# Some loads and stores of the decoder step moved from SyncE's DMA queue to GpSimd's, two blocks not fetched twice, gate weights split later

## The chip, the cores and the metric

The kernel runs on one core of a Trainium2 chip. The metric is the device time of one execution in microseconds, the median of several runs.

## What is computed

One inference step of a two-layer decoder with 2048 prompt positions and 32 sample positions (8 sequences of 4), model width 1024. Layer 0 is gated linear attention, layer 1 a sliding-window attention over one shared K/V. Cut to what matters:

```python
u = rmsnorm(h, norm_g)                       # layer 0
q, k, v, gate, g_low = split(u @ a_w_in)     # widths 512, 512, 2048, 2048, 16
log_a = log_sigmoid(g_low @ a_w_gate2 + a_b_gate) / 16
o, state = gla_recurrence(q, k, v, log_a)    # 4 heads, chunks of 64
h = h + (rmsnorm(o) * silu(gate)) @ a_w_out  # 2048 -> 1024
k, v = shared_kv(h)                          # 4 KV heads of 64
q, gate = split(rmsnorm(h, b_norm) @ b_w_in) # layer 1, 32 heads of 64
o = banded_attention(q, k, v, window=128, sinks)
y = h + (o * silu(gate)) @ b_w_out           # 2048 -> 1024
```

The same is done for the sample positions (`ys`), and the recurrent states and K/V caches are further outputs.

## The kernel before

Values are carried as pairs of 16-bit numbers (a high and a low half), so a product takes three matmul passes, and every weight is loaded raw in 32 bits, split by ScalarE (high half) and VectorE (low half) at L197 and L198, and then multiplied. Transposed operands are made by transposing DMAs, all of them on SyncE's queue.

The stages, in order of time. (1) **The start**, 0 to about 60 us: the first 512 positions of `x_prompt` are loaded (`u_steps`, L382) and normed in four chunks of 128 (`norm_T`: a square sum on ScalarE and VectorE, the reciprocal root on GpSimd as `rs_m`, `rs_r` at L186 and L187, the scaled halves into `ogT`, two transposes `uT<-ogT` at L322), the first head's weights are loaded and split (`Unit.convert`, L223), and the low-rank gate's weights `wg` are split by GpSimd (`split_wg`). (2) **Layer 0**, to about 1150 us, with 36 weights of layer 1 prepared on the side (`pre<-pst` stores on GpSimd's queue). (3) **The form stage**, about 1150 to 1410 us: `a_out` makes layer 0's output projection for 16 chunks of 128 positions. Each chunk fetches four transposed blocks (`sg<-ogd` or `v<-ogd`, L1059, the two names in turn), multiplies, adds the residual on VectorE (L1066, one half of the columns at a time, with `X` loaded at L1064), stores `hd` (L1067) and norms the chunk. Beside it `form_steps` prepares layer 1's output weights: the output projection of layer 1 takes chunks in pairs by a scheme of seven products in place of eight, for which seven combinations of four weight blocks are formed. For each of 8 steps `m` it loads four blocks of 256 KB of `b_w_out` (L857; two `wraw`, one `qT`, one `kT`, these two with one buffer each), subtracts four times on GpSimd (L864), splits seven times on ScalarE and VectorE, and stores seven results in `wfd` from GpSimd's queue (L878). (4) **Layer 1**, to about 2500 us: four groups of 16 blocks, TensorE's order written out by hand in `ORDER`. (5) **The tail**, from about 2500 us: the first products of the pairs, the sample's output (`s_out`, `b_finish_s`, L1664 to L1670), and pairs 0 to 7. A pair needs four blocks (`load`, `fetch`, transposes `<-oge` at L1569), sums of them on VectorE (`sums`: `whole` L1583, L1595, L1600, L1601, L1609), seven products of 24 matmuls, and for each of four results an `hd` load (L1625), two adds (L1626, L1618) and a store of `y` (L1627).

What sets the order: the Tile scheduler orders each engine's instructions, each engine and each DMA queue then works in that order, so an instruction that waits holds all behind it on its queue. `behind(..., 200)` lowers the priority of a list of steps; `later` is a DMA that keeps its place in the program. `trickle` and `summing` hand out single steps of the first pair's loads, weight fetches and sums between the last blocks of layer 1, and `run(trickle + summing)` does what is left of them. `wform_big` (L1533) fetches a formed weight into a `uT` buffer (four quarters of 512 KB), `wform` (L1538) into `W` buffers. Product n=6 of a pair uses weight 6, which `wform_big` fetches into the buffer `t_` that holds four blocks (0 to 3) fetched earlier for the first products.

Of the kernel before, what the change touches and what calls it, by code (L numbers as in the profile page):

```python
# [19 lines left out]
P = 128  # L20
# [54 lines left out]
def _body(tc, nc, cp, sb, ps, dr, i, o):  # L75
# [88 lines left out]
    def run(steps):  # L164
        for f in steps:
            f()
# [23 lines left out]
    def split(dst, src, sc=None, eng=dve):  # L190
# [5 lines left out]
        else:  # L196
            act(hi, src, AF.Copy, scale=sc)  # L197
            dve.scalar_tensor_tensor(lo, src, sc, hi, ALU.mult, ALU.subtract)  # L198

    class Unit:  # L200


# [9 lines left out]
        def convert(self, half, dst):  # L212

            ncol, gs = self.ncol, self.gs
            nk = 512 // ncol
            raw = T("wraw", [P, 512], F32, 3)
            for n, (off, w, src) in enumerate(self.parts):
                if self.groups:
                    g, z = self.groups, len(self.parts)
                    to = raw.rearrange("p (g z d) -> p z g d", z=z, g=g)[:, n]  # L220
                    nc.sync.dma_start(to, src[half * P : (half + 1) * P].rearrange("p (g d) -> p g d", g=g))
                    continue
                nc.sync.dma_start(  # L223
                    raw.rearrange("p (k c) -> p k c", c=ncol)[:, :, off : off + w],
                    src[half * nk * P : (half + 1) * nk * P].rearrange("(k p) c -> p k c", p=P),
                )
            if gs is None:
                split((dst(0), dst(1)), raw, SW)
                return
            for n in range(nk):  # L230
                d = slice(n * ncol, (n + 1) * ncol)
                k = self.kts[half * nk + n]
                split((dst(0)[:, d], dst(1)[:, d]), raw[:, d], gs[:, k : k + 1])
# [92 lines left out]


    wg_raw = T("E", [P, KT, RANK], F32, 2)
    nc.scalar.dma_start(wg_raw, i["a_w_in"][0, :, 5120:5136].rearrange("(k p) c -> p k c", p=P))
    wg = T("ogTs", [P, KT, 6 * RANK], F16, 1)  # L330
    w2 = T("w2", [6 * RANK, 512], F16, 1)
    gl = T("gl", [6 * RANK, NBL, 512], F16, 1)
# [516 lines left out]
    def form_steps(m):  # L849

        b, f = {}, {}

        def load():
            for n, (r, z) in enumerate(((0, 0), (0, 1), (1, 0), (1, 1))):
                t = T(("wraw", "wraw", "qT", "kT")[n], [P, 512], F32, 3 if n < 2 else 1)
                k = UP[m] + 2 * r
                nc.sync.dma_start(t, i["b_w_out"][0][k * P : (k + 1) * P, z * 512 : z * 512 + 512])  # L857
                b[r, z] = t
            f[0], f[3], f[5] = b[0, 0], b[1, 0], b[1, 1]

        def put(n):
            def sub(x, y):
                t = T("sth", [P, 512], F32, 2)
                pool.tensor_tensor(t, x, y, ALU.subtract)  # L864
                f[n] = t

            if n == 2:
                sub(b[0, 1], b[0, 0])
            elif n == 1:
                sub(b[1, 1], f[2])  # L870
            elif n == 4:
                sub(b[1, 1], b[0, 1])
            elif n == 6:
                sub(b[1, 0], f[1])
            t = T(tags[0], [P, 2, 512], F16, 2)
            tags.append(tags.pop(0))
            split((t[:, 0], t[:, 1]), f[n], SWB)
            nc.gpsimd.dma_start(wfd[n][:, m], t)  # L878

        return behind([load] + [lambda n=n: put(n) for n in (0, 2, 1, 3, 6, 5, 4)], 200)  # L880
# [26 lines left out]
    qk_chunk, qk_fin = cur.qk_first()  # L907
    first = u_steps(0)
    qkw = [f for u in hw[0].qk for f in u.steps()]
    run([first[0]] + qkw[:2] + [first[1]] + qkw[2:] + first[2:4])  # L910
    split_wg()
    run(hw[0].v.steps())
    load_w2()
# [640 lines left out]
    class Pair:  # L1554
# [66 lines left out]
        def y(self, c, half, pp, t):  # L1621

            cs = slice(half * 512, half * 512 + 512)
            hr = T("E", [P, 512], F32, 2)
            nc.sync.dma_start(hr, hd[c][:, cs])  # L1625
            dve.tensor_tensor(hr, hr, t, ALU.add)  # L1626
            nc.sync.dma_start(o["y"][0, c * P : (c + 1) * P, cs], self.add("st", pp, hr))  # L1627

        def steps(self, n):
            tag, w = PRODS[n]  # L1630
# [33 lines left out]
    def b_finish_s(half, pt):  # L1664
        cs = slice(half * 512, half * 512 + 512)
        hr = T("E", [SMP, 512], F32, 2)
        nc.sync.dma_start(hr, hsd[:, cs])
        y = T("st", [SMP, 512], F32, 2)
        dve.tensor_tensor(y, pt, hr, ALU.add)
        nc.sync.dma_start(o["ys"].flatten_outer_dims()[:, cs], y)  # L1670

    blks = []
    parts = {}
# [12 lines left out]
    for t in range(-3, NKV * NCH):  # L1686
        fill = []
        n = t + 3
# [34 lines left out]
        if n == TOT - 11:  # L1723
            t_ = T("uT", [P, 8, 8, P], F16, 4)
            for x in range(4):
                pr = pairs[x // 2]
                pr.l[x % 2] = [t_[:, 2 * x], t_[:, 2 * x + 1]]
                pr.fetch(x % 2, pr.l[x % 2])
        if n in (TOT - 7, TOT - 3):
            run(quarters(wform_big, {TOT - 7: 0, TOT - 3: 2}[n]))  # L1730
        if n == TOT - 14:
            run(quarters(wform, 3))
        if n == TOT - 1:
            trickle += [lambda x=x: pairs[0].load(x) for x in (3, 2, 0, 1)] + quarters(wform_big, 1)
            summing += pairs[0].sums()
        if n == TOT:
            trickle += quarters(wform, 4) + quarters(wform, 5)
        if n == TOT + 1:
            trickle += quarters(wform_big, 6)
        if boundary:  # L1740
            boundary.pop(0)()
    for n, (od, ca) in enumerate((("cks", "cache_swa_k"), ("cvs", "cache_swa_v"))):
# [3 lines left out]
    for n, od in enumerate(("cks", "cvs")):  # L1746
        for b in range(NS):
            nc.sync.dma_start(o[od][b, WIN - TS :], kvS[b * TS : (b + 1) * TS, n])
    run(trickle + summing)
    for p_ in range(NCH // 2):  # L1750
        more = []
        if p_ + 1 < NCH // 2:
# [91 lines left out]
```

## Time and profile before

| | |
|---|---|
| runs of before | 2858.11, 2863.62, 2863.80 us (median 2863.62) |
| profiled execution | 2863.85 us; its span 2862.1 us |
| TensorE busy | 2735.9 us, 96% |
| VectorE, ScalarE, GpSimd busy | 64%, 50%, 37% |
| mean granted TensorE clock | 0.983 of full speed |
| DMA through SyncE's and ScalarE's queues (hardware_dynamic) | 352.75 MB, 54.6% of 16 engines' span |
| DMA through GpSimd's queue (software_dynamic) | 35.66 MB, 3.4% |
| VectorE's last add ends / the span ends | 2858.8 / 2862.1 us |

The span is the time from the first to the last instruction of the profiled execution, 1.75 us shorter than that execution's own time. Share of busy time is an average; what a stage is worth is read from the stretches in which TensorE stands idle.

### The profile page before, as it was taken

Reading aid. Unit: us, or ns where it says so; the run is one execution under the profiler, and the core shown is the slowest. Engines: PE = TensorE matmul, PEld = TensorE weight load, DVE = VectorE, ACT = ScalarE, POOL = GpSimd, SP = SyncE. Lnnn points to the kernel's source line nnn. Section 1 sums busy time; section 2 is a strip of 40 time slices with the busy share of each in tenths; the row PEclk is TensorE's granted clock in tenths of the full one; section 3 lists DMA queues with packets and bytes.
Section 4 is the critical chain, followed back from the end, with each engine's and each line's share of the span. In section 5 each row is a group of like instructions: output and inputs, shape, how many; then the busy total and the mean of one; then the engine's idle time right before and its main releaser. Section 6 shows DMA issues by size and latency. Waiting matters only on the chain.

```text
span 2862.1 us, 51609 instructions
## 1 busy us (share of the span) xinstructions
PE 2735.9 (96%) x19070; PEld 1392.4 (49%) x19070; DVE 1845.7 (64%) x3815; ACT 1440.3 (50%) x3385; POOL 1063.6 (37%) x1471
## 2 busy tenths in 40 slices
PE   6899999999999999999899999999999999988999
PEld 3445444444454444444344555555555555543444
DVE  5767787677768775336413666677777766767653
ACT  6655665466546654333313555566666666641110
POOL 1242233222322321116405676666566556530000
PEclk9899999999999999999999999999999999999999
DMA  8351334124312533799975555866877788798651
GB/s 209 90 124 36 100 101 150 38 82 136 115 38 85 171 84 96 180 240 282 233 193 135 108 130 120 203 117 129 173 116 130 157 155 165 151 236 172 125 112 57
DMA packets 774230, 391.78 MB, mean 137 GB/s; under 512 B 629200, under 2 KB 698776, under 8 KB 773944
## 3 DMA queue, kind: packets, MB, share of 16 engines
q1 hardware_dynamic: 761016, 352.75, 54.6%
q0 software_dynamic: 10880, 35.66, 3.4%
q8 instruction: 149, 2.44, 0.4%
q14 instruction: 105, 0.86, 0.1%
q10 hardware_dynamic: 2080, 0.07, 0.0%
HBM read 138.90 MB, written 107.54 MB: 86 GB/s over the span
## 4 chain that ended last, share of the span: by engine, by line
PE 56%; DVE 12%; DMA 11%; ACT 10%; issue 6%; POOL 4%; SPq 1%; DVEq 0%; ACTq 0%; POOLq 0%
PE pj L101 33%; PE o L101 11%; PE tr L101 8%; PE kv L101 3%; ACT o L1279 2%; DMA pst<-v 2%; DVE v L198 2%; ACT v L197 2%; DMA pre<-pst 1%; PE lev L101 1%; DMA wraw<-in_a_w_in_dram 1%; DVE o L1274 1%; DVE W L198 1%; POOL ogT L195 1%; DVE lev L1274 1%
## 5 line engine op out<-in xcount | busy, mean ns | idle before, releaser
L101 PE MATMUL pj<-W,uT 128*128 128x512 f16 x5088 | 1208.1, 383 | 6.6 <-ACT qT L430 2.9
L101 PEld LDWEIGHTS <-uT 128*128 128x128 f16 x6976 | 654.7, 99 | 714.1 <-issue 40.4
L101 PE MATMUL tr<-W,uT 128*128 128x512 f16 x1536 | 365.8, 379 | 0.0
L186 POOL TENSOR_SCALAR rs_m<-ss 128x1 f32<-128x1 f32 (+3 forms) x190 | 46.1, 243 | 685.7 <-ACT og L611 234.0
L101 PEld LDWEIGHTS <-X 128*128 128x128 f16 x2744 | 185.8, 98 | 149.3 <-issue 14.7
L1279 ACT ACTIVATE o<-o,mx 128x256 f32<-128x256 f32 (+1 forms) x384 | 168.5, 439 | 168.1 <-DVE mx L1274 163.6
L1274 DVE CUSTOM_DVE_ANT_0 o<-o,madd,nsink 128x256 f32<-128x256 f32 (+1 forms) x384 | 184.0, 479 | 48.3 <-PE o L101 44.0
L101 PE MATMUL pj<-uT,W 128*128 128x512 f16 (+1 forms) x912 | 186.0, 354 | 27.0 <-DMA uT<-ogT 24.3
L198 DVE SCALAR_TENSOR_TENSOR v<-o,v 128x512 f16<-128x512 f32 (+1 forms) x192 | 128.8, 671 | 102.0 <-ACT v L197 82.0
L187 POOL TENSOR_TENSOR rs_r<-rs_m,mhalf 128x1 f32<-128x1 f32 (+2 forms) x186 | 184.8, 994 | 14.4
L101 PEld LDWEIGHTS <-W 128*128 128x128 f16 x2448 | 128.0, 98 | 113.1 <-issue 18.5
L101 PEld LDWEIGHTS <-v 128*128 128x128 f16 x976 | 95.2, 98 | 116.0 <-DMA v<-ogd 1.9
L508 POOL TENSOR_TENSOR E<-bt 128x256 f32<-128x256 f32 x96 | 73.9, 770 | 198.4 <-DVE X L195 124.8
L195 POOL TENSOR_TENSOR ogT<-og,ogT 128x512 f16<-128x512 f32 x68 | 88.0, 1295 | 154.4 <-ACT ogT L194 142.5
L101 PEld LDWEIGHTS <-sth 128*128 128x128 f16 x2080 | 111.4, 99 | 52.3 <-DMA sth<-v 12.2
L101 PEld LDWEIGHTS <-sg 128*128 128x128 f16 x800 | 78.6, 99 | 107.5 <-DMA sg<-ogd 12.3
L101 PE MATMUL o<-gl,X 128*128 128x256 f16 (+1 forms) x768 | 114.9, 273 | 5.5 <-DMA X<-qe 5.5
L197 ACT ACTIVATE v<-o 128x512 f16<-128x512 f32 (+1 forms) x192 | 111.3, 579 | 11.1 <-DMA sth<-v 7.6
L101 PE MATMUL kv<-rmask,sth 128*128 128x64 f16 x1984 | 107.0, 194 | 10.1 <-DMA sth<-v 9.2
L101 PE MATMUL kv<-rmask,pst 128*128 128x64 f16 x992 | 102.4, 194 | 9.3 <-DMA pst<-v 9.3
L1279 ACT ACTIVATE lev<-lev,mx 128x256 f32<-128x256 f32 (+1 forms) x128 | 56.5, 441 | 103.3 <-DVE mx L1274 101.2
L101 PE MATMUL pj<-W,v 128*128 128x512 f16 x448 | 104.2, 379 | 1.1 <-DMA v<-ogd 1.1
(468 smaller groups left out, 5092.5 us busy)
## 6 DMA issues: line engine op xcount, KB each, us to landing
pre<-pst POOLq DMA_DIRECT2D x72, 256.0 KB, 3.4
W<-pre SPq DMA_DIRECT2D x36, 512.0 KB
ogd<-ogT SPq DMA_DIRECT2D x68, 256.0 KB
wraw<-in_a_w_in_dram SPq DMA_DIRECT2D x64, 256.0 KB
wraw<-in_b_w_in_dram SPq DMA_DIRECT2D x64, 256.0 KB
oge<-ogT SPq DMA_DIRECT2D x64, 256.0 KB
wraw<-in_a_w_out_dram SPq DMA_DIRECT2D x32, 256.0 KB
X<-in_x_prompt_dram SPq DMA_DIRECT2D x32, 256.0 KB
```

The source lines that it names most:

```text
L101: return order(nc.tensor.matmul(*a, **k))
L186: pool.tensor_scalar(m[:n, :k], ss, a, b, ALU.mult, ALU.add)
L187: pool.tensor_tensor(r[:n, :k], m[:n, :k], mhalf[:n, :k], ALU.pow)
L195: eng.tensor_tensor(lo, src, hi, ALU.subtract)
L197: act(hi, src, AF.Copy, scale=sc)
L198: dve.scalar_tensor_tensor(lo, src, sc, hi, ALU.mult, ALU.subtract)
L508: pool.tensor_tensor(Ev[:, :, 0, :], ref, btv[:, :, 0, :], ALU.subtract)
L1274: dve.tensor_tensor_reduce(pm[:, z], pm[:, z], madd.rearrange("p a b -> p (a b)")[:, (2 - nk) * P :], -0.125, nsink[:, g * GRP + h : g * G ...
L1279: act(pm[:, z], pm[:, z], AF.Exp, scale=-1.0, bias=nm_[:, h : h + 1], accum_out=bx["sum"][:, h : h + 1])
```

## The change

Five edits. (a) The 32 loads of `b_w_out` in `form_steps` are issued by GpSimd in place of SyncE. (b) The `hd` loads and `y` stores of the pairs, and the `hsd` loads and `ys` stores of the sample, 68 DMAs, are issued by GpSimd too. (c) The four transposes that fetched blocks 0 and 1 of pair 0 a second time are left out; the sums read the earlier copy in `t_`. (d) `wform_big` 2 comes one block earlier, and `wform_big` 6 after the last of `trickle` and `summing`. (e) At the start the gate weight's load moves from ScalarE's queue at the beginning to SyncE's queue behind the norms, with it its split, and the first unit's weight loads keep their place in the program.

```diff
+    q_load = [nc.sync.dma_start]
...
-                nc.sync.dma_start(
+                q_load[0](
                     raw.rearrange("p (k c) -> p k c", c=ncol)[:, :, off : off + w],
...
-    nc.scalar.dma_start(wg_raw, i["a_w_in"][0, :, 5120:5136].rearrange("(k p) c -> p k c", p=P))
...
-                nc.sync.dma_start(t, i["b_w_out"][0][k * P : (k + 1) * P, z * 512 : z * 512 + 512])
+                nc.gpsimd.dma_start(t, i["b_w_out"][0][k * P : (k + 1) * P, z * 512 : z * 512 + 512])
...
-    run([first[0]] + qkw[:2] + [first[1]] + qkw[2:] + first[2:4])
+    first[0]()
+    q_load[0] = later
+    run(qkw[:2])
+    q_load[0] = nc.sync.dma_start
+    run([first[1]] + qkw[2:] + first[2:4])
+    later(wg_raw, i["a_w_in"][0, :, 5120:5136].rearrange("(k p) c -> p k c", p=P))
     split_wg()
...
-            nc.sync.dma_start(hr, hd[c][:, cs])
+            nc.gpsimd.dma_start(hr, hd[c][:, cs])
             dve.tensor_tensor(hr, hr, t, ALU.add)
-            nc.sync.dma_start(o["y"][0, c * P : (c + 1) * P, cs], self.add("st", pp, hr))
+            nc.gpsimd.dma_start(o["y"][0, c * P : (c + 1) * P, cs], self.add("st", pp, hr))
...
-        nc.sync.dma_start(hr, hsd[:, cs])
+        nc.gpsimd.dma_start(hr, hsd[:, cs])
...
-        nc.sync.dma_start(o["ys"].flatten_outer_dims()[:, cs], y)
+        nc.gpsimd.dma_start(o["ys"].flatten_outer_dims()[:, cs], y)
...
+                if x < 2:
+                    pr.r[x] = pr.l[x]
-        if n in (TOT - 7, TOT - 3):
-            run(quarters(wform_big, {TOT - 7: 0, TOT - 3: 2}[n]))
+        if n in (TOT - 7, TOT - 4):
+            run(quarters(wform_big, {TOT - 7: 0, TOT - 4: 2}[n]))
...
-            trickle += [lambda x=x: pairs[0].load(x) for x in (3, 2, 0, 1)] + quarters(wform_big, 1)
+            trickle += [lambda x=x: pairs[0].load(x) for x in (3, 2)] + quarters(wform_big, 1)
...
-        if n == TOT + 1:
-            trickle += quarters(wform_big, 6)
...
-    run(trickle + summing)
+    run(trickle + summing + quarters(wform_big, 6))
```

SyncE's queue in the form stage, kernel before, around the fetch of the blocks of the chunk that is stored as `hd_148`:

```order
L857 DMA qT_15283<-in_b_w_out_dram 128x512
L1067 DMA hd_148<-E_14537 128x512
L1064 DMA X_14707<-in_x_prompt_dram 128x512
L857 DMA kT_15285<-in_b_w_out_dram 128x512
L857 DMA wraw_15472<-in_b_w_out_dram 128x512
L1059 DMA_TRANSPOSE sg_14632<-ogd_107 128x8x128
L1059 DMA_TRANSPOSE sg_14634<-ogd_107 128x8x128
L857 DMA wraw_15474<-in_b_w_out_dram 128x512
L1059 DMA_TRANSPOSE sg_14636<-ogd_107 128x8x128
L1067 DMA hd_148<-st_14605 128x512
L1059 DMA_TRANSPOSE sg_14638<-ogd_107 128x8x128
```

The same place of SyncE's queue in the changed kernel:

```order
L1073 DMA hd_148<-E_14537 128x512
L1070 DMA X_14707<-in_x_prompt_dram 128x512
L1065 DMA_TRANSPOSE sg_14632<-ogd_107 128x8x128
L1065 DMA_TRANSPOSE sg_14634<-ogd_107 128x8x128
L1065 DMA_TRANSPOSE sg_14636<-ogd_107 128x8x128
L1073 DMA hd_148<-st_14605 128x512
L1065 DMA_TRANSPOSE sg_14638<-ogd_107 128x8x128
```

No weight load stands between the transposes any more; the store of the first half's residual still stands ahead of them. The loads are now on GpSimd's queue, among its subtractions (L865), stores and norms (L186, L187):

```order
L858 DMA kT_14856<-in_b_w_out_dram 128x512
L858 DMA wraw_15088<-in_b_w_out_dram 128x512
L879 DMA wf_133<-Sh_14830 128x1024
L858 DMA wraw_15090<-in_b_w_out_dram 128x512
L879 DMA wf_132<-Sh_14936 128x1024
L879 DMA wf_131<-qe_14894 128x1024
L865 TENSOR_TENSOR sth_14914<-kT_14856,sth_14892 128x512
```

A load stands ahead of stores that wait for splits and of subtractions that wait for loads, on one queue.

SyncE's queue in the tail, kernel before, from the fetch of weight 6 (`wf_135`) to the sample's store:

```order
L1533 DMA uT_31286<-wf_135 128x2048 x4
L1569 DMA_TRANSPOSE v_31551<-oge_116 128x8x128
L1285 DMA_TRANSPOSE sth_31199<-v_31165 128x8x128
L1285 DMA_TRANSPOSE pst_31201<-v_31166 128x8x128
L629 DMA oge_127<-ogT_31229 512x1x256
L1625 DMA E_31245<-hd_142 128x512
L1667 DMA E_31439<-hsd 32x512
...
L1627 DMA out_y_dram<-st_31248 128x512
...
L1670 DMA out_ys_dram<-st_31441 32x512
L629 DMA oge_128<-ogT_31492 512x1x256
```

The same place in the changed kernel:

```order
L1575 DMA_TRANSPOSE v_31543<-oge_116 128x8x128
L630 DMA oge_127<-ogT_31221 512x1x256
L1291 DMA_TRANSPOSE sth_31191<-v_31157 128x8x128
L1539 DMA uT_31505<-wf_135 128x2048 x2
L1291 DMA_TRANSPOSE pst_31193<-v_31158 128x8x128
L1539 DMA uT_31505<-wf_135 128x2048 x2
...
L630 DMA oge_128<-ogT_31479 512x1x256
```

The four residual DMAs are gone from this queue, and weight 6 is fetched behind the transpose `sth` and around `pst` in place of ahead of both. They stand on GpSimd's queue now, between its multiplications:

```order
L195 TENSOR_TENSOR ogT_31221<-wraw_31219,ogT_31221 128x512
L1314 TENSOR_TENSOR dn_31384<-sm_5142_31032,es_5183_31381 128x8
L1631 DMA E_31237<-hd_142 128x512
L1318 TENSOR_TENSOR sg_30819<-sg_30819,rv_31386 128x512
L1673 DMA E_31427<-hsd 32x512
L1633 DMA out_y_dram<-st_31240 128x512
L1676 DMA out_ys_dram<-st_31429 32x512
L195 TENSOR_TENSOR ogT_31479<-wraw_31477,ogT_31479 128x512
```

The last multiplication `ogT` stands behind both stores.

At the start, the first rows of SyncE's queue in the changed kernel:

```order
L383 DMA v_301<-in_x_prompt_dram 128x512
L324 DMA_TRANSPOSE uT_156<-ogT_218 128x8x128
L324 DMA_TRANSPOSE uT_156<-ogT_219 128x8x128
L108 DMA wraw_227<-in_a_w_in_dram 128x2x128 x2
L108 DMA wraw_234<-in_a_w_in_dram 128x2x128 x2
L225 DMA wraw_264<-in_a_w_in_dram 128x2x128 x2
```

Before, eight weight loads stood between the eight loads of `x`, ahead of these two transposes; now all eight loads of `x` come first, and the weights behind the transposes.

## Rows read from the trace of the kernel before

**Rows 1.** The page: share of busy time of each engine over the span.

```profile
PE 2735.9 (96%) x19070; PEld 1392.4 (49%) x19070; DVE 1845.7 (64%) x3815; ACT 1440.3 (50%) x3385; POOL 1063.6 (37%) x1471
```

**Rows 2.** Waits of PE, whole span: what ended them, us in total, times, longest.

```profile
PE pj L101 <- DMA uT<-ogT: 24.3, 7, 17.7
PE pj L101 <- DMA sg<-ogd: 10.9, 2, 9.4
```

**Rows 3.** Timeline of PE, form stage: start, us, what, [idle before <-releaser].

```profile
1384.07 1.04 PE L101 MATMUL pj<-W,sg 128*128 128x512 f16 x2 [9.36 <-DMA sg<-ogd]
```

**Rows 4.** Busy time by stretch: PE, PEld, DVE, ACT, POOL, PEclk, DMA share, GB/s.

```profile
1384.00:1391.00 7.00, 5.40 (x13) 1.74 (x14) 4.05 (x7) 3.40 (x7) 4.67 (x7) 0.50 1.18 252
2586.00:2592.00 6.00, 4.11 (x10) 1.49 (x11) 4.26 (x7) 1.17 (x2) 0.00 (x0) 0.53 1.13 255
```

**Rows 5.** Timeline of SyncE's DMA queue, form stage.

```profile
1358.23 4.94 SPq L322 DMA_TRANSPOSE uT<-ogT  x2
1363.27 0.53 SPq L857 DMA_DIRECT2D kT<-in_b_w_out_dram  x1
...
1372.75 0.33 SPq L1067 DMA_DIRECT2D hd<-E  x1
...
1375.50 5.38 SPq L1059 DMA_TRANSPOSE sg<-ogd  x2
```

**Rows 6.** Timeline of POOL and DVE, form stage.

```profile
1357.95 1.28 POOL L864 TENSOR_TENSOR sth<-kT,wraw 128x512 f32<-128x512 f32 x1
...
1369.25 1.19 DVE L198 SCALAR_TENSOR_TENSOR pst<-kT,pst 128x512 f16<-128x512 f32 x1 [5.33 <-ACT pst L197]
...
1372.05 0.68 DVE L1066 SCALAR_TENSOR_TENSOR E<-pj,X 128x512 f32<-128x512 f32 x1
```

**Rows 7.** DMA stores and loads on GpSimd's queue: issue on POOL, then us to landing.

```profile
L248 POOL DMA_DIRECT2D pre<-pst x72: 677/690/785, 414.0 to 1283.8; - x72
...
DMA to landing us min/median/max: 2.5/3.4/6.1
```

**Rows 8.** Waits of SyncE's queue, 1140 to 1420 us.

```profile
SPq L857 <- POOL sth L864: 9.3, 6, 6.7
```

**Rows 9.** Timeline of PE, tail.

```profile
2558.83 0.20 PE L101 MATMUL kv<-rmask,pst 128*128 128x64 f16 x1 [3.79 <-DMA pst<-v]
2569.34 0.59 PE L101 MATMUL pj<-uT,S 128*128 128x512 f16 x2 [0.84 <-DMA uT<-wf]
2587.89 1.03 PE L101 MATMUL tr<-W,X 128*128 128x512 f16 x2 [3.66 <-DVE st L1669]
2623.43 0.59 PE L101 MATMUL o<-W,qe 128*128 128x512 f16 x2 [4.53 <-DVE st L1618]
```

**Rows 10.** Timeline of SyncE's DMA queue, tail.

```profile
2550.07 0.55 SPq L1627 DMA_DIRECT2D out_y_dram<-st  x1
...
2552.03 2.27 SPq L1285 DMA_TRANSPOSE pst<-v  x1
...
2582.96 0.53 SPq L1627 DMA_DIRECT2D out_y_dram<-st  x1
```

**Rows 11.** Timeline of DVE, tail.

```profile
2579.33 0.69 DVE L1618 SCALAR_TENSOR_TENSOR st<-pj,E 128x512 f32<-128x512 f32 x1
...
2587.16 0.68 DVE L1669 TENSOR_TENSOR st<-tr,E 32x512 f32<-32x512 f32 x1 [5.33 <-DMA out_y_dram<-st]
...
2605.33 1.29 DVE L1583 TENSOR_TENSOR wraw<-sth,pst 128x512 f32<-128x512 f16 x2 [5.91 <-DMA pst<-oge]
```

**Rows 12.** Timeline, start: POOL, SyncE's queue.

```profile
6.78 0.61 POOL L336 TENSOR_TENSOR E<-E,gsa 128x128 f32<-128x128 f32 x1 [5.04 <-DMA E<-in_a_w_in_dram]
...
9.48 0.24 POOL L186 TENSOR_SCALAR rs_m<-ss 128x1 f32<-128x1 f32 x1
...
11.76 4.70 SPq L322 DMA_TRANSPOSE uT<-ogT  x2
```

**Rows 13.** Timeline of DVE, end.

```profile
2858.11 0.69 DVE L1618 SCALAR_TENSOR_TENSOR st<-pj,E 128x512 f32<-128x512 f32 x1 [1.82 <-PE pj L101]
```

## The prediction

> **What bounds the kernel now.** I read the page's first part first: TensorE is busy in 96% of the span [rows 1], so about 126 us of 2862.1 are gaps, and the change touches no matmul. What it can win is some of those gaps, and the slow clock behind them. Second, the waits of TensorE over the whole span [rows 2]: the largest ends on the transposes `uT<-ogT` (24.3 us, of which 17.7 are the start of the kernel), the next on `sg<-ogd` (10.9 us in two waits). Third, the timeline of TensorE in the stages the change touches. In the form stage one gap of 9.36 us ends at 1384.07 on `sg<-ogd` [rows 3]; in the tail four gaps of 0.84 to 4.53 us end on a transpose, a weight fetch and twice on VectorE [rows 9]. Fourth, the table by stretch, for the clock: in the 7 us behind the first of these gaps the granted clock is 0.50, which is the lower of the two levels, 1.2 GHz, and it is 0.53 in the 6 us around the gap of the sample's output [rows 4]. So a gap costs its own length and some time after it. Last, the queue of SyncE, to see what made the awaited transfer late: each of these is late because something unrelated waited in front of it.
>
> The sum is made against the profiled execution, 2863.85 us, which is within 0.01% of the median of the runs, 2863.62. About 0.2%, 5.7 us, is what a measurement of this kernel can tell from no change; its own runs spread that far.
>
> **The form stage (loads of `b_w_out` to GpSimd).** The chain of the 9.36 us: the single buffer `kT` is free when GpSimd's subtraction ends, 1357.95 + 1.28 = 1359.23 [rows 6]. Its next load is issued only at 1363.27, since SyncE stood at two transposes `uT<-ogT` from 1358.23 for 4.94 us [rows 5]. VectorE waits 5.33 us for that block's split and does it at 1369.25; behind it on the same engine is the residual add of the chunk, at 1372.05 [rows 6]; SyncE stores its result at 1372.75 and gets to the transposes `sg<-ogd` at 1375.50 [rows 5], with weight loads between. TensorE starts 8.6 us after that issue, at 1384.07, having been ready at 1384.07 - 9.36 = 1374.7 [rows 3].
>
> With the load on GpSimd, it goes out behind the subtraction that frees the buffer. The nearest row for its price is the `pre<-pst` store of the same 256 KB: 0.69 us to issue, 3.4 us to landing, 6.1 at most [rows 7]. So it is there at 1359.2 + 0.7 + 3.4 = 1363.3, against about 1368.5 before (1369.25 less ScalarE's half of the split, about 0.7 as VectorE's row of the same block size [rows 13]): 5 us earlier, 2.5 with the slowest landing. The residual and its store come 5 us earlier with it. Between that store and the transposes lie 1375.50 - 1372.75 = 2.75 us, most of them weight loads that are gone from the queue; I take 2. So the transposes start 7 us earlier, and the gap falls from 9.36 to about 2.4. Of the second wait, 10.9 - 9.4 = 1.5 us [rows 2], I take 0.5, as one load between the transposes is gone. The clock: 5.40 us of matmuls ran at 0.50 in that stretch [rows 4], 2.7 at full clock, so 2.7 us to be had, and I take 2.5. Sum **10 us**. Upper bound: both waits and the clock, 10.9 + 2.7 = 13.6. Lower bound: below nothing, -8, worked out as a rival. I take a value near the top because every link of the chain is a row.
>
> What it costs GpSimd: 32 issues of 0.69, 22 us over a stage of 250 us; its subtractions cover none of TensorE's time. A load that waits for its buffer now holds the stores, subtractions and norms behind it. SyncE waited for such buffers 9.3 us in six waits, 6.7 at the longest, on GpSimd's subtraction [rows 8]; these cost nothing on GpSimd itself, which by then has done the subtraction.
>
> **The tail.** (1) The `y` store at 2550.07 stands two fetches ahead of the transpose `pst<-v` at 2552.03 [rows 10], which ends the gap of 3.79 [rows 9]. The changed queue has no store there and the transposes in a row: 2552.03 - 2550.07 = 2 us earlier, gain **2**. (2) VectorE ends a `y` add at 2580.02 [rows 11], SyncE stores it only at 2582.96 [rows 10], since it was busy with transposes; the buffer `st` comes free after that, and the sample's add at 2587.16 had waited 5.33 us for it [rows 11], and TensorE 3.66 us for the add [rows 9]. GpSimd stores at once: 2582.96 - 2580.02 = 2.9 us earlier, less some 0.4 us of its slower issue, gain **2.5**. The 4.11 us of matmuls at 0.53 there [rows 4] would be 2.2 at full clock; of the 1.9 I take **1**, as a gap of 1.2 us is left. (3) The gap of 4.53 [rows 9] hangs on VectorE, which ran without a break from a landing `pst<-oge` at 2605.33 [rows 11]. That transpose still stands behind the sample's last steps and the two cache copies on SyncE. It comes some 3 us earlier, but so does TensorE: I take **1** of 4.53. (4) Four transposes are not issued, some 2 us each by the row of `pst<-v` (2.27 [rows 10]): 8 us of SyncE's time between other work, of which I take **1**. (5) A loss: weight 6 is fetched behind one more transpose (2.3 us by the same row) and into a buffer that is free later, since the sums of pair 0 now read it. TensorE waited 0.84 for it before [rows 9] and comes up to 3 us earlier now; some of its matmuls are put off behind other work. I take **-3.5**, with 0 and -8 as ends (the second: 2.3 + 3 and about 2.7 for a landing at the slow end, 6.1 - 3.4 [rows 7]). Sum of the tail 2 + 2.5 + 1 + 1 + 1 - 3.5 = **4 us**, between -5 (the loss of 8 against 3 of the gains) and 13 (2 + 3.66 + 1.9 + 4.53 + 1).
>
> **Start, end and the rest.** The first norm stood on GpSimd behind the gate's split, from 6.78 to 9.48 us [rows 12]; that is up to 2.7 us to be had. Against it the first weights now go out behind two transposes, which took 4.70 [rows 12]. One unit's weights have to land and be split before the first matmul, so I take **0**, with +2.7 and -4.7 as ends. Weight 2's earlier fetch and the gate's later split are costed at nothing: the first goes to a buffer no row shows as awaited, the second runs on GpSimd, which waits for loads at that time (5.04 us [rows 12]); without that cover it costs its 2.7 us. At the end, after the last add at 2858.11 [rows 13], only the store is left; GpSimd's issue of 0.69 and landing of 3.4 [rows 7] make 4.1 us against 2862.1 - 2858.8 = 3.3: **-1**. The remaining loads and stores of the pairs, some 60, go to GpSimd, which is at 0.00 busy in the tail's row [rows 4].
>
> Sum: 10 + 4 + 0 - 1 = 13, so 2863.85 - 13 = **2850.9**, said as 2851.
>
> **Rivals.** (a) **The transfers are late because the DMA engines are full**, whoever issues them. For it: the DMA share is 1.18 and 1.13 in the two rows of the half clock [rows 4]. Against it: the chain above shows 4 us of pure queueing (1359.23 to 1363.27) before the transfer exists. Then the form stage gives 1 and the tail 2.5 - 1: 2861, no change. (b) **GpSimd becomes the queue that holds**: in the form stage a load waits there for a split that frees `qT` or `kT`, the norm of a chunk (`rs_m`) waits behind it, so `uT<-ogT` on SyncE waits, and the next chunk's transposes stand behind those. One such hold as long as SyncE's longest, 6.7 us [rows 8], in two chunks is 13.4; with the 2.7 of clock, less 8 that the loads still save, that is a loss of 8 in place of the gain of 10: 2863.85 + 8 - 4 + 1 = 2869, slower. It decides from a hold of more than the 9.36 us by which the transposes were late, in one chunk's four loads. Against it: its buffers are freed mostly by GpSimd's own work. (c) **GpSimd's issue and landings stretch** when VectorE works beside it. In the rows issue is 0.677 to 0.785 and landing 2.5 to 6.1 us [rows 7], while VectorE is at 58% of the stretch [rows 4]. With each decisive landing at 6.1 in place of 3.4, the form stage gives 2.7 less and the end costs 2.7 more: 2856. The Trainium skill, DMA: Bandwidth & Descriptors, section SWDGE vs HWDGE vs iDMA, has the rule that speaks against this change: descriptors of GpSimd's DMAs are written by software into rings in SBUF, which VectorE locks GpSimd out of in some modes, and DMAs of SyncE are immune. By that rule the issue would stretch; the trace shows it steady, within 0.11 us over 72 stores. (d) **All waits named go, and none comes**: 13.6 + 13 + 2.7 - 1 = 28: 2836.
>
> **How the numbers follow.** The forecast has 0.50, (a) 0.16, (b) 0.10, (c) 0.07, (d) 0.17. The range runs from just below (d), 2834, to 2866, between (a) and (b); it leaves out part of (b) and what lies beyond the unknown start. Faster by over 0.2%, below 2858: (d), nearly all of the forecast and (c), 0.74; within 0.2%: (a) and the forecast's upper end, 0.16; slower: (b), 0.10.
>
> **What would show it.** Right: no wait of PE on `sg<-ogd` over 3 us near 1384 and full clock behind it; `kT` landing within 5 us of the subtraction that frees it; the gap on the sample's add down to about 1 us; a longer wait of PE on `uT<-wf`; the last store 4 us after the last add. Wrong: the same gap on `sg<-ogd` with the loads landing early (a); waits of SyncE or ScalarE on `rs_r`, and of GpSimd on VectorE before a load (b); issues over 0.8 us on GpSimd (c); a first matmul later than 18 us. The prediction as a whole is wrong above 2866 or below 2834.

## The result and the profile after

The changed kernel takes 2871.02 us (median of 11 runs, 2863.05 to 2879.91), the kernel before 2861.63 in the same comparison (11 runs, 2857.72 to 2872.61): a ratio of 1.0031, 95% interval 1.0016 to 1.0047, so about 9 us slower. Run again later on another occasion, it was 1.0025 (1.0004 to 1.0047). The forecast was 2851, faster; the direction was wrong and the time lies outside the range.

One warning before the profile is read. The profiled execution of the changed kernel took 2863.05 us, the fastest of its eleven; a second profiled execution of the same program, below, spans 2884.5. That one is the slowest of its twelve. A kernel that waits on transfers is not told by one trace, neither this one nor the one of before.

The page of the changed kernel, first part; busy time per engine hardly moves, but GpSimd has 53 us more ([rows 1]), its hundred new DMA issues:

```profile
PE 2732.3 (95%) x19070; PEld 1389.5 (49%) x19070; DVE 1843.7 (64%) x3815; ACT 1437.4 (50%) x3385; POOL 1117.0 (39%) x1571
```

Timeline of PE, with the rows that answer to [rows 3] and [rows 9], and three of the start:

```profile
15.96 3.52 PE L101 MATMUL pj<-uT,W 128*128 128x128 f16 x36 [15.96 <-ACT W L197]
...
62.63 5.73 PE L101 MATMUL pj<-W,uT 128*128 128x512 f16 x18 [3.35 <-DVE v L198]
...
73.56 0.59 PE L101 MATMUL pj<-uT,W 128*128 128x512 f16 x1 [3.73 <-DVE E L513]
...
1384.54 4.92 PE L101 MATMUL pj<-W,sg 128*128 128x512 f16 x22 [1.59 <-DMA sg<-ogd]
...
1408.00 11.73 PE L101 MATMUL pj<-W,v 128*128 128x512 f16 x46 [6.87 <-DMA v<-ogd]
...
2537.90 1.03 PE L101 MATMUL o<-gl,X 128*128 128x256 f16 x4 [2.30 <-DMA X<-qe]
...
2561.41 0.72 PE L101 MATMUL lev<-ogTs,uT 128*128 128x64 f16 x16 [3.23 <-DVE v L198]
...
2569.34 0.59 PE L101 MATMUL pj<-uT,S 128*128 128x512 f16 x2 [2.49 <-DMA uT<-wf]
...
2619.80 1.01 PE L101 MATMUL o<-W,qe 128*128 128x512 f16 x2 [4.84 <-ACT X L194]
```

The gap of 9.36 on `sg<-ogd` is 1.59 here and the sample's add holds nobody; but the next chunk waits 6.87 on `v<-ogd`, weight 6 is waited for 2.49 in place of 0.84, two new gaps stand in the tail, and the start has gaps of 3.35 and 3.73 behind VectorE. The clock did come back in the old place and went in the new (busy time by stretch, columns as in [rows 4]):

```profile
1384.00:1391.00 7.00, 6.46 (x30) 2.95 (x31) 5.63 (x8) 3.68 (x8) 5.39 (x7) 1.00 1.01 323
1390.00:1410.00 20.00, 13.13 (x61) 5.94 (x60) 8.01 (x13) 5.93 (x13) 10.28 (x16) 0.86 1.12 199
```

### The profile page after: what moved, and what is told of

It is laid out like the page before. It is cut to its first block, busy times and chain, and to the rows that moved or that the text cites. A ratio compares the mean times of both kernels' runs of the same rounds, so it can differ in the third digit from the quotient of the medians.

```text
span 2861.3 us, 51565 instructions
## 1 busy us (share of the span) xinstructions
PE 2732.3 (95%) x19070; PEld 1389.5 (49%) x19070; DVE 1843.7 (64%) x3815; ACT 1437.4 (50%) x3385; POOL 1117.0 (39%) x1571
## 4 chain that ended last, share of the span: by engine, by line
PE 58%; DMA 11%; DVE 11%; ACT 9%; issue 6%; POOL 4%; SPq 1%; POOLq 0%; DVEq 0%; ACTq 0%
PE pj L101 34%; PE o L101 11%; PE tr L101 8%; PE kv L101 3%; ACT o L1285 2%; DMA pre<-pst 2%; PE lev L101 2%; DVE v L198 2%; DMA pst<-v 1%; ACT v L197 1%; DMA wraw<-in_a_w_in_dram 1%; DVE o L1280 1%; DMA uT<-ogT 1%; POOL ogT L195 1%; DVE lev L1280 1%
## 5 line engine op out<-in xcount | busy, mean ns | idle before, releaser
L186 POOL TENSOR_SCALAR rs_m<-ss 128x1 f32<-128x1 f32 (+3 forms) x190 | 45.5, 239 | 653.4 <-ACT og L612 243.0
L187 POOL TENSOR_TENSOR rs_r<-rs_m,mhalf 128x1 f32<-128x1 f32 (+2 forms) x186 | 186.7, 1004 | 14.5
```

Of the source, the lines that this page charges most:

```text
L186: pool.tensor_scalar(m[:n, :k], ss, a, b, ALU.mult, ALU.add)
L187: pool.tensor_tensor(r[:n, :k], m[:n, :k], mhalf[:n, :k], ALU.pow)
```

## The experiments

All ratios are against the kernel before, run on the same chip in the same comparison (medians 2858 to 2860 us there), so 0.0010 is 2.9 us.

### One part at a time

The diffs are those parts of the change that their names say. **Start alone** (edit e):

> The kernel before with the start of the change alone (x loads first, gate weights behind the norms). Theory S, the changed kernel lost its time in the first 200 us (its profiled execution reaches the product that the kernel before starts at 358.75 us only at 362.73): 5 to 9 us slower than before. Theory F (GpSimd's queue in the form stage costs the time) and theory W (weight 6 and the sums' buffer in the tail): within 2 us of before.

Measured 1.0011 (0.9999 to 1.0023), 3 us, at the edge of what can be told; at the product that before starts at 200 us it is 5.6 us late.

**Loads of `b_w_out` on GpSimd alone** (edit a):

> The kernel before with the loads of b_w_out on GpSimd's queue alone; TensorE's order is the same. Theories S and W: 3 to 10 us faster, the wait of TensorE on sg<-ogd of 9.36 us mostly gone. Theory F: 5 us slower or more, with new waits of TensorE on v<-ogd or sg<-ogd in 1350 to 1450 us of over 9 us together.

Measured 0.9977 (0.9962 to 0.9992): 6.6 us faster. Its profile is the fastest of its twelve runs, 15 us below their median; in it neither `sg<-ogd` nor `v<-ogd` is waited for over 0.4 us in 1350 to 1450. Busy time from 1350 to 1420 before and in this run (columns as in [rows 4]):

```profile
1350.00:1420.00 70.00, 57.97 (x258) 25.26 (x257) 35.84 (x42) 23.27 (x45) 37.55 (x46) 0.90 0.98 258
```

```profile
1350.00:1420.00 70.00, 70.00 (x330) 32.06 (x328) 32.14 (x41) 21.37 (x42) 40.09 (x57) 1.00 1.01 242
```

**Residual DMAs on GpSimd alone** (edit b):

> The kernel before with the residual loads and result stores of the pairs and of the sample on GpSimd's queue alone. Theories S and F: 2 to 4 us faster, the wait of TensorE on the sample's add (3.66 us) under 1.5 us. Theory W: the same, since weight 6 keeps its place. A rival, GpSimd's queue holds multiplications and stores in the tail: 2 to 5 us slower, with TensorE waits that end on a chain from GpSimd.

Measured 1.0040 (1.0025 to 1.0056): 11.4 us slower, more than any theory named. In its profile the last add of VectorE ends earlier than before (2854.33 against 2858.80); but the span ends at 2865.2, 10.8 us behind that add in place of 3.3. The last DMA issue on GpSimd, and what the kernel's closing line shows for GpSimd (DRAIN rows: min/median/max in ns, first and last start):

```profile
2854.62 0.54 POOL L1627 DMA_DIRECT2D out_y_dram<-st  x1 [3.68 <-DVE st L1618]
```

```profile
L1840 POOLq DRAIN  x3: 40/98/9791, 2854.6 to 2864.9; - x3
```

GpSimd drains its queue at the end of the program, here for 9.79 us. No transfer is under way for most of it: the last bytes of `y` move before 2858, and the DMA share is 0.00 from there to the end. Before, the drain has the same place in the program but begins at 2582.5, with GpSimd idle since, and nobody sees it:

```profile
L1840 POOLq DRAIN  x3: 40/102/4879, 2582.5 to 2861.8; - x3
```

**Blocks not loaded twice, weights 2 and 6 moved** (edits c and d):

> The kernel before with the two blocks not loaded twice and the weights 2 and 6 in their new places. Theory W: 4 to 6 us slower, the wait of TensorE on uT<-wf of 0.84 us grown to 3 us or more. Theories S and F: within 2 us of before.

Measured 1.0006 (0.9993 to 1.0019): no difference that can be told. Its profile is 4.9 us later at the product that before starts at 2583, counted from 2500; at 2590 it is level again (0.2 earlier), since the wait of 3.66 on the sample's add [rows 9] is not there. Its wait on `uT<-wf` is 2.62.

### The drain at the end

```diff
+            q = nc.gpsimd if c == NCH - 1 and half == 0 else nc.sync
-            nc.sync.dma_start(o["y"][0, c * P : (c + 1) * P, cs], self.add("st", pp, hr))
+            q.dma_start(o["y"][0, c * P : (c + 1) * P, cs], self.add("st", pp, hr))
```

> The kernel before with one DMA moved: the very last store of y is issued by GpSimd in place of SyncE; nothing else changes on any engine. Theory D (GpSimd drains its queue at the end of the program, 4 to 10 us in the profiles; with its last DMA long past, the drain is hidden, with its last DMA at the end, it is exposed): 4 to 9 us slower, with the end of the span 8 us or more behind the last add. Theory Q (the 68 moved DMAs cost time where they are issued, in the tail): at most 1 us slower, the dearer issue of one DMA.

Measured 1.0020 (1.0007 to 1.0032): 5.7 us for one moved DMA. The drain is 4.42 us in its profile and the span ends 5.5 us after the last add (theory D said 8 or more), against 3.3 before: 2.2 us of the 5.7 are seen there; the rest is within the interval.

The changed kernel with the last pair back on SyncE:

```diff
+            q = nc.sync if self.p == NCH // 2 - 1 else nc.gpsimd
-            nc.gpsimd.dma_start(hr, hd[c][:, cs])
+            q.dma_start(hr, hd[c][:, cs])
...
-            nc.gpsimd.dma_start(o["y"][0, c * P : (c + 1) * P, cs], self.add("st", pp, hr))
+            q.dma_start(o["y"][0, c * P : (c + 1) * P, cs], self.add("st", pp, hr))
```

> The changed kernel with the loads and stores of the last pair (eight DMAs) back on SyncE's queue. Theory D: 5 to 9 us faster than the changed kernel, that is within 3 us of the kernel before, and the drain on GpSimd ends before the last add. Theory Q: under 1.5 us faster than the changed kernel, still 7 us slower than before.

Measured 1.0018 (1.0005 to 1.0032): 2 to 4 us better than the change, less than theory D said, and the intervals overlap. In the change's own profile the drain is short, 3.83 us, and the span ends 4.9 us after the last add, which is 1.6 more than before:

```profile
L1846 POOLq DRAIN  x3: 46/98/3834, 2856.6 to 2861.0; - x3
```

The same edit on parts a and b together, and on b alone:

> The kernel before with the loads of b_w_out on GpSimd, and the residual DMAs of all but the last pair. Theory D: 5 to 9 us faster than before (the 6 of the form stage alone and what the residual DMAs give without the drain). Theory Q: no faster than before, since the residual DMAs' cost of 10 us stays and eats the 6.

> The kernel before with the residual DMAs of all but the last pair on GpSimd's queue. Theory D (of the residual part's loss, the exposed drain at the end is the greater share): within 2.5 us of before, with the span ending 3 to 4 us after the last add. Theory Q (the moved DMAs cost time in the tail themselves): 4 us slower or more, and the distance from the product at 2500 us to the last one grown by 3 us or more.

Measured 1.0005 (0.9990 to 1.0020) and 1.0007 (0.9992 to 1.0021). With its drain hidden (9.14 us long, from 2825.5), the residual part went from 11.4 us to 2, which cannot be told from nothing: the drain was most of it. But the 6 of the loads did not show beside it.

### One program, two executions

> The changed kernel unchanged, for a second profiled execution and times on this chip. Theory D: 8 to 10 us slower than before; if the drain at the end is 8 us or more in this execution, in place of the 3.8 of the first profile, the span is 5 us longer at the end alone. Theory Q: as slow, with a drain of 4 us and the loss in the stages ahead of it.

Measured 1.0025 (1.0004 to 1.0047), runs from 2851.11 to 2886.32. The drain was 3.84 us again, so theory D's guess of 8 was wrong; of the 23 us between the two profiled executions 17 lie in the form stage and 4 in the tail. Timeline of PE in the second:

```profile
1384.88 5.35 PE L101 MATMUL pj<-W,sg 128*128 128x512 f16 x24 [1.84 <-DMA sg<-ogd]
1396.22 7.62 PE L101 MATMUL pj<-W,sg 128*128 128x512 f16 x22 [5.98 <-DMA sg<-ogd]
1422.36 6.94 PE L101 MATMUL pj<-W,v 128*128 128x512 f16 x24 [6.86 <-DMA v<-ogd]
1431.29 6.61 PE L101 MATMUL pj<-W,v 128*128 128x512 f16 x22 [1.98 <-DMA v<-ogd]
```

And the chain, read up from the load: GpSimd's timeline, VectorE's, SyncE's queue.

```profile
1382.52 0.57 POOL L858 DMA_DIRECT2D kT<-in_b_w_out_dram  x1
...
1395.45 1.27 POOL L865 TENSOR_TENSOR sth<-kT,sth 128x512 f32<-128x512 f32 x1 [7.53 <-DMA kT<-in_b_w_out_dram]
...
1396.14 1.13 DVE L198 SCALAR_TENSOR_TENSOR pst<-kT,pst 128x512 f16<-128x512 f32 x1 [9.06 <-ACT pst L197]
...
1398.13 0.68 DVE L1072 SCALAR_TENSOR_TENSOR E<-pj,X 128x512 f32<-128x512 f32 x1
...
1398.84 0.33 SPq L1073 DMA_DIRECT2D hd<-E  x1
...
1404.97 9.89 SPq L1065 DMA_TRANSPOSE v<-ogd  x3
```

It is the very chain of the prediction, link by link: the load of `kT`, the split, the residual add behind it on VectorE, its store, the transposes behind the store (with two transposes `uT<-ogT` between them this time). Only the load, issued at once, lands 12.9 us after its issue began (1382.52 to about 1395.4), not 3.4. Issue to landing of GpSimd's loads in the first profile of the change, and in this one:

```profile
DMA to landing us min/median/max: 3.2/6.2/12.0
```

```profile
DMA to landing us min/median/max: 3.3/7.3/17.1
```

### Is it the queue, the buffer, or the DMA engines?

Loads on ScalarE's queue (`nc.scalar.dma_start` in that one line):

> The kernel before with the loads of b_w_out on ScalarE's queue in place of SyncE's. Theory L (the gain of the form stage is SyncE's queue relieved, and the long landings of GpSimd's loads, 5.5 us in the middle and up to 17, take part of it back): 8 to 14 us faster than before, landings shorter than on GpSimd's queue. Rival H (ScalarE's waits for free buffers hold its splits): no faster than before, with ScalarE waiting in front of the loads and new waits of TensorE on sg<-ogd or v<-ogd.

Measured 1.0082 (1.0062 to 1.0101): 23 us slower. That it is no faster is what rival H said, but what ScalarE stands at longest are late landings: of the loads, and of the `wf` stores that free the buffers of its splits. Timeline of ScalarE and of SyncE's queue:

```profile
1381.33 0.33 ACTq L857 DMA_DIRECT2D qT<-in_b_w_out_dram  x1
...
1390.56 0.63 ACT L197 ACTIVATE qe<-qT 128x512 f16<-128x512 f32 x1 [7.12 <-DMA qT<-in_b_w_out_dram]
1390.58 0.34 ACTq L857 DMA_DIRECT2D wraw<-in_b_w_out_dram  x1
```

```profile
1381.79 9.98 SPq L1059 DMA_TRANSPOSE sg<-ogd  x2
```

A load issued at 1381.33 is there by 1390.56 on this queue, and two transposes beside it take 9.98 us in place of 5.38 [rows 5]. The `wf` stores, which stay on GpSimd's queue in this run, land at 7.8 us at the median, against 5.4 before. So landing late is no trait of loads on GpSimd's queue. That the DMA engines are full is argued, not shown, as the reason: from 1350 to 1420 their share of busy time is 0.98 before, 1.11 and 1.08 in the two profiles of the change and 1.12 here, but also 1.01 with the loads alone on GpSimd, where no product waits.

A second buffer for the awaited blocks, with the loads on GpSimd, and on SyncE:

```diff
-                t = T(("wraw", "wraw", "qT", "kT")[n], [P, 512], F32, 3 if n < 2 else 1)
+                tag = ("wraw", "wraw", "bt", "bt")[n] if m % 2 else ("wraw", "wraw", "qT", "kT")[n]
+                t = T(tag, [P, 512], F32, {"wraw": 3, "bt": 2}.get(tag, 1))
```

> The kernel before with the loads of b_w_out on GpSimd and with the single buffers qT and kT taken in turn with bt's, so that a step's loads go out while the step before is still being split. Theory L (late landings of the single-buffered blocks are what VectorE, ScalarE and GpSimd stand at): 8 to 14 us faster than before, every wait of TensorE on sg<-ogd and v<-ogd under 2 us. Rival: the landings are late because the DMA engines are full, and more loads in flight only land later: no faster than the loads on GpSimd alone (6 us).

> The kernel before with the same second buffers, its loads still on SyncE's queue. Theory L: 4 to 10 us faster than before, since a load that SyncE issues late is no longer waited for. If SyncE's place in the queue is what counts and not the buffer: within 2 us of before, the wait on sg<-ogd still 6 us or more.

Measured 1.0039 (1.0016 to 1.0061), slower, with runs from 2851 to 2890; and 0.9978 (0.9967 to 0.9989), faster, with runs from 2846 to 2861. On GpSimd the extra loads in flight land later (longest 17.3 us) and hold the transposes: in its profile TensorE waits 3.31 and 5.01 us on `v<-ogd`.

```profile
1362.79 12.73 PE L101 MATMUL pj<-W,v 128*128 128x512 f16 x46 [5.01 <-DMA v<-ogd]
```

On SyncE the same buffers are a gain. Our reading, which no run tests by itself, is that the queue that issues the transposes also spaces the loads, and a second buffer takes the split off the chain. The wait on `sg<-ogd` is 4.30 us, between the two theories; it decides nothing, since with single buffers on SyncE that wait was 2.10 to 9.36 us in ten profiles.

### The parts inside the change

> The changed kernel with the loads of b_w_out back on SyncE's queue. Theory G (in the changed kernel the form stage gives its 6 us only in executions where GpSimd's loads land early, so on the mean it gives little): within 3 us of the changed kernel, 5 to 9 us slower than before, and a narrower spread of its runs. Theory A (the parts add up): 12 to 16 us slower than before.

> The changed kernel with the start of before. Theory A (the parts add up, the start costs 3 us): 3 us faster than the changed kernel, 4 to 6 us slower than before, and 3 to 7 us earlier than the changed kernel at the product that before starts at 200 us. If the start costs nothing: as slow as the changed kernel.

Measured 1.0040 (1.0026 to 1.0054) and 1.0007 (0.9988 to 1.0026). Without the start the change is 5 to 7 us faster, though the intervals overlap. Without the GpSimd loads it is 2.6 to 4.3 us slower, between theories G and A; yet the drain of this program, exposed at the end, is 9.79 us against 3.83, which is 6 us that have nothing to do with the form stage. Inside the change the GpSimd loads gain nothing there that shows. They went with a wider spread, as theory G expected: 10.6 us from the fastest to the slowest run without them, 17 and 35 in the two comparisons of the change. Over all programs here it is 17 to 38 us with the loads on GpSimd and 10 to 18 with them on SyncE.

Which half of the start:

```diff
-    nc.scalar.dma_start(wg_raw, i["a_w_in"][0, :, 5120:5136].rearrange("(k p) c -> p k c", p=P))
...
     run([first[0]] + qkw[:2] + [first[1]] + qkw[2:] + first[2:4])
+    later(wg_raw, i["a_w_in"][0, :, 5120:5136].rearrange("(k p) c -> p k c", p=P))
```

> The kernel before with one half of the start edit: the gate weight's load and split behind the norms, the first unit's weight loads between the loads of x as before. Theory X (the first unit's weights behind the transposes cost the time): within 2 us of before or up to 3 us faster, and at the product that before starts at 200 us no later than before. Theory Y (the late gate costs it, since the decays of the first block wait for it at 60 to 100 us): 3 to 6 us slower, 4 to 7 us late at 200 us.

Measured 1.0025 (1.0011 to 1.0039): the late gate costs 7 us, theory Y and a little more. It does what it is for: the first matmul starts at 13.01 us, 4.7 earlier than before. But the gate's split is done from 34.93 in place of 6.78 [rows 12], and the products that wait for it come later too (timelines of POOL and PE):

```profile
34.93 0.40 POOL L335 TENSOR_TENSOR E<-E,gsa 128x128 f32<-128x128 f32 x1 [15.29 <-DMA E<-in_a_w_in_dram]
```

```profile
42.88 3.62 PE L101 MATMUL tr<-uT,ogTs 128*96 128x512 f16 x16
53.02 0.38 PE L101 MATMUL tr<-gl,w 96*128 96x512 f16 x1
```

The second of these was at 47.25 before and is at 48.54 in the change. Behind it come the decays of the first block; the scan that makes them starts 4 us later than before (timeline of DVE, before and in this run), and by 200 us this program is 6.5 us late and the change 7.6.

```profile
60.20 1.22 DVE L372 TENSOR_TENSOR_SCAN bt<-rmask,E 128x512 f32<-128x512 bf16 x1
```

```profile
64.17 1.22 DVE L371 TENSOR_TENSOR_SCAN bt<-rmask,E 128x512 f32<-128x512 bf16 x1
```

### The tail

Weight 6 alone behind the sums; and the blocks alone not loaded twice:

> The kernel before with the fetch of weight 6 alone put behind the last sums; the two blocks are loaded twice as before. Theory W6 (the late fetch is what loses time at 2550 to 2590 us in every profile that has it): TensorE is 4 us or more later at the product that the kernel before starts at 2590 us, counted from 2500, with a wait on uT<-wf of 2 us or more; the whole time 2 to 4 us slower. Theory T (the order that the missing loads bring is what loses it): no loss there.

> The kernel before with the two blocks not loaded twice, weights 2 and 6 fetched at their places of before. Theory W6: no loss from 2500 to 2590 us, 0 to 3 us faster than before. Theory T: 4 us later at 2590, counted from 2500, and 2 to 4 us slower.

Measured 0.9999 (0.9984 to 1.0013) and 0.9998 (0.9985 to 1.0011), both neutral. Theory W6 fell: the late fetch alone loses nothing (1.7 us earlier at 2583, counted from 2500). Nor does theory T stand as it was put (4 us late at 2590, 2 to 4 slower): with the loads left out the profile is 5.4 us late at 2583, but 0.4 at 2590, behind the place where before waits for the sample's add, and the whole time is the same. The eight profiled executions with edit c gain 2.8 us on the mean between 1480 and 2500 (the twelve others 0.2) and lose 3.6 from 2500 to the last product (the others gain 0.5). What it gains ahead it gives back in the tail. There TensorE waits for VectorE, which works through sums and splits without a break, and the second wait shown here (3.22 to 3.41 us) stands in all eight profiles with edit c and in none of the others. From the profile of the missing loads alone:

```profile
2541.27 0.23 PE L101 MATMUL kv<-rmask,sth 128*128 128x64 f16 x2 [3.82 <-DVE E L1583]
...
2556.90 0.80 PE L101 MATMUL lev<-ogTs,uT 128*128 128x64 f16 x16 [3.41 <-DVE v L198]
```

### A version that beats both

> The kernel before with the second buffers for qT and kT, loads on SyncE's queue, and the two blocks not loaded twice. From the parts (6 us faster, and neutral): 4 to 8 us faster than before; faster than the changed kernel by 11 us or more. If the second buffers' gain was chance: within 3 us of before.

Measured 0.9981 (0.9967 to 0.9994): 5.4 us faster than before and some 13 faster than the change. The second buffers on SyncE's queue hold up; the loads not made add nothing.

## Why the prediction was wrong

Where the time went, from the traces: start of the same matmul, by its number in TensorE's order, less its start in the profile of before, as what is lost in each stretch (us; "end" is from the last product to the end of the span):

```
                           to 600  600-1350  1350-1480  1480-2500  2500-last  end
change, first profile       +2.4     +0.2       -5.2       -1.9       +2.1   +1.6
change, second profile      +3.4     +0.3      +11.9       -0.6       +5.8   +1.6
start alone                 -0.1     +0.3       +0.3       +2.2       -2.4   +0.0
loads alone                 -3.0     -4.4      -15.1       -0.8       -1.3   +0.0
residual DMAs alone         -3.9     +0.7       -3.0       +0.0       +1.8   +7.6
change, last pair on SyncE  -0.1     +2.9      -15.7       -4.8       +3.7   +0.0
change without the loads    +2.5     -0.7       -5.4       -3.9       +4.0   +7.6
change without the start    -3.5     +3.4       -7.2       +0.4       +5.0   +1.6
```

A stretch that an edit does not touch moves too from one execution to the next, by 4 us (the residual DMAs alone, to 600) and by 7 (the late gate alone gains 7.1 from 1350 to 1480), so single cells carry little; the verdicts are the ratios above.

The forecast was 13 us faster and 9 slower was measured; no one step makes up the 22.

**The form stage, forecast 10 us gained: the mechanism was right, the size failed.** The step is the price of the load: "3.4 us to landing, 6.1 at most", taken from the `pre<-pst` stores [rows 7]. The loads landed in 6.2 and 7.3 us at the median and 12 and 17 at most. (The profile counts a landing from the start of the issue, so the sum's 0.69 stands in it twice; that is small, and the other way.) In the two profiled executions of the change the stretch gained 5.2 and lost 11.9; in the six with GpSimd loads and single buffers it ran from 15.7 gained to 11.9 lost. The stores that gave the price ran from 414 to 1284 us, nearly all ahead of the part in which transposes, loads and stores of formed weights come together. A nearer row was there: the 56 `wf` stores of the kernel before, also 256 KB on GpSimd's queue, all but one of them from 1289 to 1405 us.

```profile
DMA to landing us min/median/max: 2.9/5.4/8.1
```

From 1359.23 its median gives an arrival at 1364.6 and its longest one at 1367.3, where the sum had 1363.3: 1.3 to 4 us less gained. In the second profile of the change the load of the chain took 12.9, longer than any of these rows. The second error is the sum's zero: the gap of 9.36 belongs to one execution; in nine other profiles with the loads on SyncE the stretch is 7.1 us shorter to 2.8 longer, 2.3 shorter on the mean, and the gap itself is 2.10 to 8.57. Rival (a), transfers late whoever issues them, deserved more than its 0.16: the loads on ScalarE's queue show it on a third queue, though not that full engines are the reason.

**The start, forecast 0 with -4.7 to +2.7: the sign and a term failed.** The first norm came earlier, as worked out (6.40 in place of 9.48). The weights behind the transposes hold the first product (15.96 in the change, 13.01 with the late gate alone), but did no harm to the whole time that shows. The error was to cost the gate's later split at nothing because GpSimd "waits for loads at that time": GpSimd had the time, but the products and decays behind the split had not. Cost 3 us alone (interval from nothing to 6.6), 7 for the gate's half, 5 to 7 inside the change.

**The end, forecast 1 us.** The step priced an issue and a landing (4.1 us against 3.3) and left out that GpSimd has work after its last issue. The store itself was quick: its bytes had moved by 2859, 2.6 us after the last add of the change. The end cost 1.6 us in the change and 7.6 with part b alone. No row of the kernel before named the drain's cost, but its row was there, 4.88 us long at an idle time.

**The tail, forecast 4 gained.** Its steps mostly held: the wait on the sample's add is gone (2.5 forecast), though it is gone in the programs with edit c alone as well, so the moved store is not the only thing that removes it; the one of 4.53 stayed, at 4.84; that on weight 6 grew from 0.84 to 2.49 and 3.72, a loss of 1.7 and 2.9 where 3.5 was set down. What failed is that nothing was set down for what comes late next: VectorE's sums, at 3.23 us in both profiles of the change. The stretch lost 2.1 and 5.8 us.

**The rivals.** (b), GpSimd as the queue that holds, is the mechanism of the second profile (GpSimd stood 7.53 us at `kT` with `rs_r` behind it), though by a late landing and not by a buffer in use. (c): the issue of the loads stayed at 0.55 us (0.546 to 0.637). The rule of the Trainium skill on GpSimd's rings (DMA: Bandwidth & Descriptors, section SWDGE vs HWDGE vs iDMA), by which VectorE in some modes locks GpSimd out of the memory that it writes descriptors to, shows nowhere in these issues. The landings did stretch, but on ScalarE's queue as well.

What stays open: start 3 to 4, form stage 5 gained on the mean of the profiles, blocks 1 to 2, end 2, residual DMAs elsewhere 2 make about 3 to 5 us; 7 to 9 are measured. The intervals (1.1 to 13.5 over both comparisons) hold both. The 5 is likely too much: the six profiled executions behind it ran 3.7 us below their programs' medians on the mean, the nine with the loads on SyncE 0.1 above. By the ratios the loads gave 6.6 us alone, 0.6 beside the residual DMAs and nothing inside the change. With 0 to 1 gained in the form stage the sum is 7 to 10.

## What to carry to other kernels

Price a transfer from rows of the stretch it will run in: the same 256 KB took 3.4 us at the median in one stage and 5.4 to 7.3 in the next, 17 at most. Moving the issues to another queue gained 6.6 us alone, nothing that shows inside the change, and lost 23 on a third queue, while a second buffer on the old queue gained 6. Look at what an engine still has to do after its last instruction before giving it the program's last DMA. And take two profiled executions where waits on transfers are the subject: one gap of 9 us may be the execution, not the kernel.

## What the runs showed of the hardware

The drain of GpSimd's queue went with the program and not with the execution: 3.83 us in both profiles of the change and in its version without the start's edit, 4.88 in before and the programs that move no DMA to GpSimd, 4.42 with one moved, 7.49 in both with 32, 9.14 with 60, 9.79 in both with 68, 3.51 in both with 92. By the number of DMAs that GpSimd issued in the program it is 4.88 (136), 4.42 (137), 7.49 (168), 9.14 (196), 9.79 (204), 3.51 (228), 3.83 (236): a figure for each number, not one rising line. Why it falls between 204 and 228 was not tried. It went on long after the last byte had moved (before, GpSimd's last store had landed by 1412 and the drain ran from 2582.5), and no cost shows where GpSimd's last issue ended 38 us or more before the end.
